# Two-layer decoder trunk on one core: four kinds of small product done another way, four small loads moved, and a new list of issue

## The chip, the core and the metric

The kernel runs on one core of one Trainium2 chip. The metric is the device time of one execution in microseconds (us). The core's engines work side by side, each through its own queue in strict order: TensorE (PE in the profile; PEld is its weight load), VectorE (DVE), ScalarE (ACT), GpSimd (POOL) and SyncE (SP, which here only issues loads and stores). DMA engines move the data between device memory and the core.

## What is computed

256 tokens of width 1024 go through two layers in f32. Cut to what matters:

```python
c_act = silu(c)
for layer in range(2):
    ada = c_act @ w_ada[layer] + b_ada[layer]              # 1024 -> 3 * 1024
    shift, scale, gate = split(ada, 3)
    h = rms_norm(x, norm_g[layer]) * (1 + scale) + shift
    if layer == 0:   # "even": two groups of eight heads
        proj = h @ w_in_even                               # 1024 -> 2840
        oa = sliding_window_attention_with_sinks(...) * silu(za)
        k_cmp, v_cmp = compress_mlp(kc), compress_mlp(vc)  # blocks of 32 tokens, stride 16: 15 blocks
        p_cmp = masked_softmax(q @ k_cmp.T * 64 ** -0.5)   # the compressed scores
        ob = (g0 * (p_cmp @ v_cmp) + g1 * selected_blocks(...) + g2 * window(...)) * silu(zb)
        y = concat(oa, ob) @ w_out_even
    else:            # "odd": sixteen heads; with 256 tokens one block, plain causal attention
        q, k, v, z = split(h @ w_in_odd, 4)                # 1024 -> 4096
        y = (causal_attention(q, k, v) * silu(z)) @ w_out_odd
    x = x + gate * y
return rms_norm(x, final_g)
```

## The kernel before

Tokens are two tiles of 128, the width eight tiles of 128. A projection is done in f32 accuracy with the faster f32r products: ACT casts a weight or an activation to f32r (`whi`, `hhi`, `ghi`), DVE subtracts it from the original to get the rest (`wlo`, `hlo`, `glo`), and `mm3` adds three products (hi·hi, hi·lo, lo·hi). So each weight tile of 128x512 costs an ACT cast, a DVE subtraction and PE products. Weights come through a ring of five tiles `raw` of 128x2048, loaded by SP.

Shift, scale and gate of a layer come from `c_act @ w_ada`, in two ways. With n = 2, `ada_sums` lets DVE multiply and add eight k-tiles of 512 columns into `acc` [128x512], whose sum over the 128 partitions is then still to be taken on PE: by `ada_shift_scale` into columns (one value to a partition, `shs`), by `ada_gate` into `gate`, broadcast over all partitions. With n = 1, `ada_rows` takes column-tiled products with `cz` (each column tile of 32 holds one value in its first column) into four partial rows, copied to `asb`, which are then summed over the four on PE. A column-tiled product uses 32 columns of the PE array; four of them run at four places of the array (`tile_position`). There are three n = 2 and two n = 1 jobs of shift and scale for layer 1, three n = 2 gate jobs (one for layer 0, two for layer 1) and two n = 1 gates. Layer 0's shift and scale belong to the start: SP loads pieces of `w_ada` into spare tiles (`qT`, `gate`, `t`), `start_sums` multiplies them on PE by `cz`, ACT copies to `asb`, PE transposes, DVE adds the bias to `shs`, then ACT and DVE scale the normalized, transposed x (`xT` in `bigA`) to `hhi` and `hlo`, and the first projection product can go. `xs` is x, loaded in two halves of 128 tokens; ACT takes each half's mean square, DVE and POOL its root.

`compress()` computes the two small networks of the compressed keys and values: partial sums in four column tiles are copied to `hp`, summed over the four on PE, and copied to `hx`. `cmp_softmax()` takes the scores of all heads against the compressed keys `kcbd`.

The order of all work is written out: `Plan.record` notes every operation with what it depends on, and `issue()` emits them in the order of the list `ORDER`. Each engine does its operations in that order. All operations are issued from one line of `record`, so the profile gives line L257 for all of them, and tiles tell them apart. PSUM has eight banks: three `ps_pj`, two `ps_s`, one each of `ps_pt`, `ps_o` and `ps_m`; the small products of the change all go to the one `ps_m`.

Of the kernel before, what the change touches and what calls it, by code (L numbers as in the profile page):

```python
# [13 lines left out]
P = 128  # L14
D = 1024
S = 256
# [252 lines left out]
def tile_trunk(  # L269
# [192 lines left out]
    def ada_shift_scale(l, g, n, a=None, st=None):  # L462
# [7 lines left out]
        for q in range(2 * n):  # L470
            T.matmul(pc[:, 2 * q : 2 * q + 2], a[:, q * P : (q + 1) * P], st[:, 0:2], start=True, stop=True)
# [902 lines left out]
```

## Time and profile before

| what | value |
|---|---|
| time, median of 3 runs | 305.65 us (305.29 to 306.19) |
| profiled execution | 306.59 us, span 304.8 us |
| PE busy | 292.1 us, 96% of the span |
| DVE busy | 260.4 us, 85% |
| ACT busy | 185.6 us, 61% |
| POOL busy | 10.7 us, 4% |
| DMA | 71.83 MB, mean 236 GB/s |
| granted PE clock | 0.999 |

The span is the profile's; 1.8 us of the profiled execution lie outside it. PE's busy time is modelled from the starts of its pipelined products. The DMA share is the mean busy share of the 16 DMA engines; it can come out a little over 1.

### The profile page before, as it was taken

The numbers are of one execution on the slowest core, as the hardware profiler recorded it, in microseconds if no ns is written. First come the engines' busy times: TensorE is split into PE (matmuls) and PEld (weight loads), VectorE is DVE, ScalarE is ACT, GpSimd is POOL, SyncE is SP. The second block draws the span as 40 slices with busy tenths as digits, with TensorE's granted clock in tenths as the row PEclk, the third lists the DMA queues.
The fourth block names the chain that finished last, engine by engine and source line by source line (L and its number), as shares of the span: only waits on it lengthen the run. The fifth ranks groups of instructions, "written<-read, shape, count | busy, mean of one in ns | idle before, by whom it ended". The sixth has DMA issues, their size and how long they took to land.

```text
span 304.8 us, 6307 instructions
## 1 busy us (share of the span) xinstructions
PE 292.1 (96%) x2303; PEld 250.3 (82%) x2303; DVE 260.4 (85%) x706; ACT 185.6 (61%) x487; POOL 10.7 (4%) x33
## 2 busy tenths in 40 slices
PE   6599999999999999999999999999999999999991
PEld 6478888898788788877877799999789989887891
DVE  0467998999999999999989887778877989999993
ACT  1662464885688978973556844474568258592532
POOL 2400000002000000000020000000000000000010
PEclk9999999999999999999999999999999999999999
DMA  7999999983997775949796958809587565342003
GB/s 253 374 309 366 387 398 378 333 281 98 308 351 236 246 247 165 364 139 301 246 303 214 298 196 268 284 19 326 199 259 236 167 248 153 125 140 69 0 2 139
DMA packets 60926, 71.83 MB, mean 236 GB/s; under 512 B 2840, under 2 KB 52448, under 8 KB 60896
## 3 DMA queue, kind: packets, MB, share of 16 engines
q1 hardware_dynamic: 60320, 70.91, 70.5%
q10 hardware_dynamic: 448, 0.48, 0.5%
q8 instruction: 18, 0.29, 0.4%
q14 instruction: 12, 0.10, 0.1%
q0 software_dynamic: 128, 0.05, 0.1%
HBM read 70.38 MB, written 1.05 MB: 234 GB/s over the span
## 4 chain that ended last, share of the span: by engine, by line
PE 87%; DVE 6%; ACT 3%; DMA 2%; issue 1%; SPq 0%; POOL 0%; ACTq 0%; DVEq 0%
PE ps_pj L257 52%; PE ps_s L257 12%; PE ps_pt L257 8%; PE ps_m L257 8%; PE ps_o L257 7%; DVE t L257 2%; DMA xs<-in_x_dram 2%; DVE wlo L257 2%; ACT t L257 1%; DVE xs L257 1%; ACT whi L257 1%; ACT L257 0%; SPq L257 0%; DVE shs L257 0%; ACT hhi L257 0%
## 5 line engine op out<-in xcount | busy, mean ns | idle before, releaser
L257 ACT CAST whi<-raw 128x512 fp32r<-128x512 f32 (+1 forms) x132 | 74.1, 600 | 19.9 <-PE ps_pj L257 11.9
L257 DVE TENSOR_TENSOR wlo<-raw,whi 128x512 fp32r<-128x512 f32 (+1 forms) x116 | 72.6, 659 | 4.6 <-ACT whi L257 4.6
L257 PE MATMUL ps_pj<-hhi,whi 128*128 128x256 f32 x256 | 68.8, 290 | 0.0
L257 PE MATMUL ps_pj<-hhi,wlo 128*128 128x256 f32 x256 | 67.7, 286 | 0.0
L257 PE MATMUL ps_pj<-hlo,whi 128*128 128x256 f32 x256 | 67.0, 284 | 0.0
L257 PEld LDWEIGHTS ps_pj<-hhi,whi 128*128 128x128 f32 x256 | 46.3, 188 | 1.5 <-issue 0.6
L257 PEld LDWEIGHTS ps_pj<-hhi,wlo 128*128 128x128 f32 x256 | 46.4, 189 | 0.5 <-issue 0.2
L257 PEld LDWEIGHTS ps_pj<-hlo,whi 128*128 128x128 f32 x256 | 46.0, 188 | 1.0 <-issue 0.7
L257 DVE SCALAR_TENSOR_TENSOR acc<-raw,cz,acc 128x512 f32<-128x512 f32 x42 | 31.3, 745 | 0.2
L257 ACT ACTIVATE sm<-sm,mn 128x256 f32<-128x256 f32 (+1 forms) x58 | 26.2, 452 | 8.4 <-DVE mn L257 8.2
L257 DVE SCALAR_TENSOR_TENSOR wlo<-raw,whi 128x512 fp32r<-128x512 f32 x32 | 21.3, 688 | 6.1 <-ACT whi L257 6.1
L257 PE MATMUL ps_pj<-whi,hhi 128*128 128x512 f32 (+2 forms) x72 | 25.8, 375 | 0.6 <-ACT hhi L257 0.6
L257 PE MATMUL ps_pj<-wlo,hhi 128*128 128x512 f32 (+2 forms) x72 | 25.9, 372 | 0.0
L257 PE MATMUL ps_pj<-whi,hlo 128*128 128x512 f32 (+2 forms) x72 | 25.7, 367 | 0.0
L257 PE MATMUL ps_pj<-wlo,ghi 128*128 128x512 f32 (+1 forms) x56 | 20.4, 367 | 0.0
L257 PE MATMUL ps_pj<-whi,ghi 128*128 128x512 f32 (+1 forms) x56 | 20.4, 370 | 0.0
L257 PE MATMUL ps_pj<-whi,glo 128*128 128x512 f32 (+1 forms) x56 | 20.2, 367 | 0.0
L257 ACT COPY pT<-ps_pt 128x384 f32<-128x384 f32 x25 | 11.9, 476 | 12.3 <-PE ps_pt L257 12.1
L257 PE MATMUL ps_pt<-ta,sm 128*128 128x128 f32 x87 | 17.4, 282 | 0.0
L257 PEld LDWEIGHTS ps_pj<-whi,hhi 128*128 128x128 f32 x72 | 13.3, 189 | 2.4 <-ACT hhi L257 1.0
L257 PEld LDWEIGHTS ps_pj<-wlo,hhi 128*128 128x128 f32 x72 | 13.4, 189 | 2.2 <-issue 0.2
L257 PEld LDWEIGHTS ps_pj<-whi,hlo 128*128 128x128 f32 x72 | 13.4, 189 | 1.7 <-DVE hlo L257 0.3
(234 smaller groups left out, 610.6 us busy)
## 6 DMA issues: line engine op xcount, KB each, us to landing
raw<-in_w_in_odd_dram SPq DMA_DIRECT2D x16, 1024.0 KB, 6.0
raw<-in_w_ada_dram SPq DMA_DIRECT2D x28, 512.0 KB, 6.7
raw<-in_w_in_even_dram SPq DMA_DIRECT2D x5, 1024.0 KB, 9.8
raw<-in_w_in_even_dram SPq DMA_DIRECT2D x7, 652.0 KB, 6.5
t<-in_w_ada_dram SPq DMA_DIRECT2D x16, 256.0 KB, 6.1
raw<-in_w_out_even_dram SPq DMA_DIRECT2D x4, 1024.0 KB, 6.7
raw<-in_w_out_odd_dram SPq DMA_DIRECT2D x4, 1024.0 KB, 5.6
qT<-in_w_ada_dram SPq DMA_DIRECT2D x12, 256.0 KB, 7.2
```

The source lines that it names most:

```text
L257: self.ops.append(dict(key=eng.key, deps=deps, fn=lambda: getattr(real, name)(*args, **kw)))
```

## The change

It makes six edits in the code and replaces the list:

1. Four small loads (the rows of `b_ada` and `norm_g`, the position rows of the two compress networks; 24, 8, 8 and 8 KB) go out on ACT's queue instead of POOL's.
2. `ada_shift_scale`, n = 2: four f32 products of `acc` tiles with two columns of ones become four column-tiled f32 products with `acc` as the moving side, a copy on ACT to `asb` and one transpose.
3. `ada_shift_scale`, n = 1: two f32 products with `sel` become two transposes and a DVE reduce over the four partial rows.
4. `ada_gate`, n = 2: one f32 product with `ones` becomes a cast on ACT, a subtraction on DVE and two f32r products with `ones_r`. Hi and rest stand in unused parts of `ghi` and `glo`, for one gate of layer 1 in `hhi` and `hlo`. POOL makes `ones_r` once.
5. `compress`: two f32 products with `sel` and a copy become two transposes and a DVE reduce.
6. `cmp_softmax`: eight f32 products of 32 columns become four column-tiled ones of 256 columns, a copy on ACT, and two transposes.
7. `ORDER` is another list throughout: 3,110 operations instead of 3,093.

```diff
@@ ORDER
-73 23 30 27 998 2 1 8 3 4 0 10 43 44 11 12 13 22 14 5 15 45 16 82 17 77 58 7 18 59 76 46 33 19 48 49 60 79 78 47
+74 23 30 27 999 2 0 8 22 10 11 1 12 13 14 3 4 5 6 7 34 15 76 80 59 35 60 75 79 84 77 36 37 16 78 61 17 44 18 38
...
@@ tile_trunk
-    G.dma_start(rows[16:64, :], b_ada.rearrange("l (k p) -> (l k) p", p=P))
+    A.dma_start(rows[16:64, :], b_ada.rearrange("l (k p) -> (l k) p", p=P))
...
@@ ada_shift_scale
-        st = st if st is not None else ones if n == 2 else sel
-        pc = bank("m")
-        for q in range(2 * n):
-            T.matmul(pc[:, 2 * q : 2 * q + 2], a[:, q * P : (q + 1) * P], st[:, 0:2], start=True, stop=True)
-        pv = pc[:, 0 : 4 * n].rearrange("p (s j e) -> p s j e", s=2, e=2)[:, :, :, 0]
+        if n == 2:
+            pa = bank("m")
+            plan.group([
+                T.matmul(
+                    pa[32 * q : 32 * q + 32, :P],
+                    ones[:, 0:32],
+                    a[:, q * P : (q + 1) * P],
+                    start=True,
+                    stop=True,
+                    tile_position=(0, 32 * q),
+                )
+                for q in range(4)
+            ])
+            asb = sb([P, 2 * P], "asb", 2)
+            A.copy(asb[:, :P], pa[:, :P])
+            pc = bank("m")
+            T.transpose(pc[:, :P], asb[:, :P], ident)
+            pv = pc[:, :P].rearrange("p (s j e) -> p s j e", s=2, e=32)[:, :, :, 0]
+        else:
+            pc = bank("m")
+            for q in range(2):
+                T.transpose(pc[:, q * P : (q + 1) * P], a[:, q * P : (q + 1) * P], ident)
+            fs = sb([P, 2], "fs", 2)
+            V.tensor_reduce(fs, pc[:, 0 : 2 * P].rearrange("p (s q e) -> p s q e", s=2, e=32)[:, :, :, 0], axis=mybir.AxisListType.X, op=ALU.add)
+            pv = fs.rearrange("p (s j) -> p s j", j=1)
...
@@ ada_gate
+        if n == 2:
+            ar = [w_[:, 0:2, :] if l and h else w_[:, 6:8, :] for w_ in ((hhi, hlo) if l and h else (ghi, glo))]
+            ar = [w_.rearrange("p a s -> p (a s)") for w_ in ar]
+            A.copy(ar[0], a)
+            V.tensor_tensor(ar[1], a, ar[0].bitcast(F32), ALU.subtract)
         pc = bank("m")
         if n == 2:
-            T.matmul(pc, ones, a, start=True, stop=True)
+            for e in range(2):
+                T.matmul(pc, ones_r, ar[e], start=e == 0, stop=e == 1)
...
@@ compress
-                T.matmul(ph[:, 32 * j : 32 * j + 32], hp[:, j * P : (j + 1) * P], sel, start=True, stop=True)
+                T.transpose(ph[:, j * P : (j + 1) * P], hp[:, j * P : (j + 1) * P], ident)
             hx = sb([P, 64], "hx", 2)
-            V.tensor_copy(hx, ph[:, :64])
+            V.tensor_reduce(hx.rearrange("p (j b) -> p j b", j=2), ph[:, : 2 * P].rearrange("p (j q b) -> p j b q", j=2, q=4), axis=mybir.AxisListType.X, op=ALU.add)
...
@@ cmp_softmax
+        pq = bank("m")
+        plan.group([
+            T.matmul(pq[32 * j : 32 * j + 32, :S], kcbd[:, j // 2, :], qbT[:, j, :], start=True, stop=True, tile_position=(0, 32 * j))
+            for j in range(4)
+        ])
+        sT = sb([P, 2 * P], "asb", 2)
+        A.copy(sT, pq[:, :S])
         pc = bank("m")
         for t in range(2):
-            for hp_ in range(4):
-                T.matmul(
-                    pc[:, t * P + 32 * hp_ : t * P + 32 * hp_ + 32],
-                    qbT[:, hp_, t * P : (t + 1) * P],
-                    kcbd[:, hp_ // 2, :],
-                    start=True,
-                    stop=True,
-                )
+            T.transpose(pc[:, t * P : (t + 1) * P], sT[:, t * P : (t + 1) * P], ident)
```

What the new list does is seen in the engines' queues. A row is an instruction (line, operation, output <- inputs, size); a number behind a tile's name is its buffer, and the buffers have other numbers after.

The first place is the head of ACT's queue, where `crow` is c, `ta` a table with the identity, `tiny` a step of silu(c), and `r` the mean squares of the two halves of x. Before:

```order
L257 DMA ta<-in_tbl_a_dram 128x160
L257 DMA crow<-in_c_dram 8x128
L257 ACT_TABLE_LOAD
L257 ACTIVATE t_86,r_85<-xs 128x1024
L257 ACTIVATE t_88,r_85<-xs 128x1024
L257 ACTIVATE t_87<-xs,r_85 128x512
L257 ACTIVATE tiny_84<-ps_pt_83 128x8
L257 CAST whi_108<-raw_100 128x512
L257 ACTIVATE t_89<-xs,r_85 128x512
L257 COPY bigA<-ps_s_91 128x4x128
```
After:

```order
L258 DMA crow<-in_c_dram 8x128
L258 DMA ta<-in_tbl_a_dram 128x160
L258 DMA rows<-in_b_ada_dram 48x128
L258 DMA rows<-in_norm_g_dram 16x128
L258 DMA rows_pe<-in_cmp_pe_k_dram 16x128
L258 DMA rows_pe<-in_cmp_pe_v_dram 16x128
L258 ACT_TABLE_LOAD
L258 ACTIVATE t_89,r_86<-xs 128x1024
L258 ACTIVATE tiny_85<-ps_pt_84 128x8
L258 ACTIVATE t_87,r_86<-xs 128x1024
L258 ACTIVATE t_90<-xs,r_86 128x512
L258 ACTIVATE t_88<-xs,r_86 128x512
```
Four loads now stand ahead of the first square (the `ACTIVATE` of 128x1024), silu(c) stands between the two squares and not behind both, and a weight cast (`CAST whi`) that stood between the two scalings of x has gone to a later row. The first square in the list after is of the other half of `xs` than before (`t` and `xs` are named alike for both halves).

SP's queue at the same place. Before:

```order
L257 DMA qT_97<-in_w_ada_dram 128x2x256
L257 DMA xs<-in_x_dram 128x1024 x2
L257 DMA raw_100<-in_w_in_even_dram 128x792
L257 DMA qT_99<-in_w_ada_dram 128x2x256
L257 DMA qT_98<-in_w_ada_dram 128x2x256
L257 DMA gate<-in_w_ada_dram 128x2x256
L257 DMA qT_99<-in_w_ada_dram 128x2x256
L257 DMA qT_97<-in_w_ada_dram 128x2x256
L257 DMA qT_98<-in_w_ada_dram 128x2x256
L257 DMA gate<-in_w_ada_dram 128x2x256
L257 DMA raw_100<-in_w_in_even_dram 128x384
L257 DMA raw_100<-in_w_in_even_dram 128x512
```
After:

```order
L258 DMA qT_98<-in_w_ada_dram 128x2x256
L258 DMA xs<-in_x_dram 128x1024 x2
L258 DMA qT_99<-in_w_ada_dram 128x2x256
L258 DMA gate<-in_w_ada_dram 128x2x256
L258 DMA qT_98<-in_w_ada_dram 128x2x256
L258 DMA qT_100<-in_w_ada_dram 128x2x256
L258 DMA raw_101<-in_w_in_even_dram 128x384
L258 DMA qT_99<-in_w_ada_dram 128x2x256
L258 DMA qT_100<-in_w_ada_dram 128x2x256
L258 DMA gate<-in_w_ada_dram 128x2x256
L258 DMA raw_101<-in_w_in_even_dram 128x512
L258 DMA raw_101<-in_w_in_even_dram 128x792
```
The load of 792 columns of `w_in_even`, third kind in the queue before, now stands behind all eight pieces of `w_ada`.

The second place is PE just ahead of the first adaLN products (`ps_m<-qT,cz` and `ps_m<-gate,cz`); `ps_m<-ones` are products of ones with no use but to keep PE at work, and `ta` is the identity of the transposes. Before (the adaLN products are the next row):

```order
L257 MATMUL ps_s_90<-ta,t_87 128x128 x2
L257 MATMUL ps_s_91<-ta,t_87 128x128 x2
L257 MATMUL ps_m_67<-ones 128x128
L257 MATMUL ps_pt_83<-ta,rows 128x64
L257 MATMUL ps_s_91<-ta,t_87 128x128
L257 MATMUL ps_pj_92<-ta,t_89 128x128
L257 MATMUL ps_s_90<-ta,t_87 128x128
L257 MATMUL ps_pj_92<-ta,t_89 128x128 x2
L257 MATMUL ps_s_91<-ta,t_87 128x128
L257 MATMUL ps_pj_92<-ta,t_89 128x128
L257 MATMUL ps_s_90<-ta,t_87 128x128
L257 MATMUL ps_m_67<-ones 128x128
```
After:

```order
L258 MATMUL ps_pt_84<-ta,rows 128x64
L258 MATMUL ps_m_67<-ones 128x128 x2
L258 MATMUL ps_pj_93<-ta,t_90 128x128 x2
L258 MATMUL ps_m_67<-ones 128x128
L258 MATMUL ps_pj_94<-ta,t_90 128x128 x2
L258 MATMUL ps_s_91<-ta,t_88 128x128 x2
L258 MATMUL ps_pj_93<-ta,t_90 128x128
L258 MATMUL ps_s_91<-ta,t_88 128x128 x2
L258 MATMUL ps_m_67<-qT_98,cz 32x128 x8
L258 MATMUL ps_m_67<-qT_99,cz 32x128 x8
L258 MATMUL ps_m_67<-qT_100,cz 32x128 x8
L258 MATMUL ps_m_67<-gate,cz 32x128 x8
```
Before, twelve transposes of the normalized x (`t`) stand ahead of the adaLN products, after nine; the products of ones stand ahead of the transposes now, and `rows` is transposed ahead of them.

The third place is DVE around layer 0's n = 2 gate (`mn` are minima of scores, `rc` and `mc`, `dc` parts of softmax). Before:

```order
L257 ISA bigA,mn_132<-ps_s_90,tb 128x256
L257 ISA mn_132 128x1
L257 ISA bigA,mn_132<-ps_s_90,tb 128x128
L257 ISA mn_132 128x1
L257 TENSOR_TENSOR t_89<-t_89,mc_159 128x256
L257 TENSOR_SCALAR sm_123<-sm_123,rc_139 128x128
L257 TENSOR_TENSOR gate<-ps_m_67,gate 128x512
L257 ISA bigA,mn_132<-ps_s_91,tb 128x256
L257 ISA mn_132 128x1
L257 TENSOR_TENSOR wlo_112<-raw_104,whi_108 128x512
```
After:

```order
L258 TENSOR_TENSOR glo<-acc_106,ghi 128x512
L258 TENSOR_SCALAR mc_160<-mc_160 128x16
L258 ISA bigA,mn_133<-ps_s_92,tb 128x128
L258 ISA mn_133 128x1
L258 TENSOR_TENSOR t_90<-t_90,mc_160 128x256
L258 TENSOR_TENSOR wlo_114<-raw_105,whi_110 128x512
L258 RECIPROCAL rc_141<-den_138 128x4
L258 ISA bigA,mn_133<-ps_s_92,tb 128x256
L258 ISA mn_133 128x1
L258 TENSOR_REDUCE dc_161<-t_90 128x16
L258 TENSOR_TENSOR rc_141<-rc_141,gt 128x4 x2
L258 TENSOR_TENSOR gate<-ps_m_67,gate 128x512
```
The subtraction `glo<-acc` is new, and `gate<-ps_m` follows eleven rows behind it, with other work of the attention and of the weights between.

More of the change, by code (lines that the diff above doesn't have):

```diff
@@ L329, in tile_trunk @@
     A.dma_start(ta, tbl_a)
-    G.dma_start(rows[16:64, :], b_ada.rearrange("l (k p) -> (l k) p", p=P))
-    G.dma_start(rows[0:16, :], norm_g.rearrange("l (k p) -> (l k) p", p=P))
-    G.dma_start(rows_pe[0:16, :], cmp_pe_k.rearrange("o (i t) d -> (o i) (t d)", t=2))
-    G.dma_start(rows_pe[16:32, :], cmp_pe_v.rearrange("o (i t) d -> (o i) (t d)", t=2))
+    A.dma_start(rows[16:64, :], b_ada.rearrange("l (k p) -> (l k) p", p=P))
+    A.dma_start(rows[0:16, :], norm_g.rearrange("l (k p) -> (l k) p", p=P))
+    A.dma_start(rows_pe[0:16, :], cmp_pe_k.rearrange("o (i t) d -> (o i) (t d)", t=2))
+    A.dma_start(rows_pe[16:32, :], cmp_pe_v.rearrange("o (i t) d -> (o i) (t d)", t=2))
     ident = ta[:, 0:128]
@@ L460, in ada_sums, with ada_shift_scale @@
                 V.scalar_tensor_tensor(a, wk, ck, a, op0=ALU.mult, op1=ALU.add)
-    def ada_shift_scale(l, g, n, a=None, st=None):
+    def ada_shift_scale(l, g, n, a=None):
         gs = slice(g, g + n)
@@ L479, in ada_shift_scale @@
             V.tensor_tensor(shs[:, l, 1, gs], shs[:, l, 1, gs], ng, ALU.mult)
+    ones_r = const([P, P], "ones_r", F32R)
+    G.tensor_copy(ones_r, ones)
     selbc = const([P, P], "selbc")
```

259 rows, old and new, of the table ORDER are left out of this document.

## The prediction

> **What bounds the kernel now.** I read the views from the coarse to the fine: first the chain that ended last, then the waits of PE, then the table of stretches, then the timelines of the places that the change touches. The chain's shares by engine:
>
> ```profile
> PE 87%; DVE 6%; ACT 3%; DMA 2%; issue 1%; SPq 0%; POOL 0%; ACTq 0%; DVEq 0%
> ```
>
> PE carries it. All waits of PE in the whole run (engine, tile, releaser, us in total, times, longest):
>
> ```profile
> PE ps_s L257 <- DVE t L257: 4.7, 1, 4.7
> PE ps_m L257 <- DVE ones L257: 1.1, 1, 1.1
> PE ps_pj L257 <- ACT hhi L257: 0.6, 1, 0.6
> ```
>
> The three lie before the first projection product at 19.82 us (rows below). From there on PE is shown to wait for nothing until its last product. The stretches tell how near the next engine stands. Columns: window, length, then busy us and instructions of PE, PEld, DVE, ACT and POOL, granted clock, DMA share, GB/s.
>
> ```profile
> 0.00:20.00 20.00, 13.48 (x109) 11.55 (x110) 5.01 (x17) 8.32 (x16) 5.32 (x23) 1.00 0.93 318
> 20.00:60.00 40.00, 40.00 (x280) 33.89 (x280) 35.78 (x77) 21.46 (x53) 0.00 (x0) 1.00 1.05 368
> 60.00:152.00 92.00, 92.00 (x790) 75.97 (x789) 90.14 (x305) 69.93 (x212) 1.59 (x3) 1.00 0.77 248
> 152.00:165.00 13.00, 12.92 (x87) 9.27 (x85) 11.65 (x29) 6.91 (x16) 1.82 (x3) 1.00 0.84 262
> 165.00:240.00 75.00, 75.00 (x577) 68.41 (x577) 60.05 (x145) 45.06 (x107) 0.67 (x1) 1.00 0.71 227
> ```
>
> So there are three regimes. Up to 19.8 us PE waits for a chain of loads, norm and adaLN sums. From 60 to 152 us PE is full and DVE idles only 92.00 − 90.14 = 1.9 us: whatever shortens PE there must also shorten DVE, or DVE takes over. From 165 to 240 us DVE idles 15 us and PE alone decides. At the border of the layers, the chain runs through DVE:
>
> ```profile
> 160.13 1.20 DVE wlo L257 x2
> 161.33 1.28 DVE t L257 x4
> ```
>
> **The change, part by part. The start.** The chain of the start, in rows of the chain, of ACT, PE and SP (start us, us, what):
>
> ```profile
> 1.74 6.33 DMA xs<-in_x_dram
> 8.09 1.06 ACT L257 ACTIVATE t<-xs 128x1024 f32<-128x1024 f32 x1 [4.93 <-DMA xs<-in_x_dram]
> 8.08 0.37 SPq L257 DMA_DIRECT2D gate<-in_w_ada_dram  x1
> 10.94 1.11 PE L257 MATMUL ps_s<-ta,t 128*128 128x128 f32 x4 [4.74 <-DVE t L257]
> 18.09 0.27 ACT L257 COPY asb<-ps_m 128x128 f32<-128x128 f32 x1 [2.40 <-PE ps_m L257]
> 19.82 0.50 PE L257 MATMUL ps_pj<-whi,hhi 128*128 128x512 f32 x1 [0.58 <-ACT hhi L257]
> ...
> DMA to landing us min/median/max: 4.2/5.3/6.3
> ```
>
> The last line is of the two loads of `xs`: the one issued second lands at 1.74 + 6.33 = 8.07, the other, with the minimum of 4.2 us and its issue half a microsecond sooner, at about 5.4. Before, ACT's first Square is of the half that lands last; the new list puts the other one first. ACT has six DMA issues and a table load ahead of it (0.45 to 0.62 and 1.28 us here), so I take 6.1 us for its start. From the Square to the first transpose it is 10.94 − 8.09 = 2.85 us, so the first transpose is at about 8.9. From there to the first projection it is 19.82 − 10.94 = 8.9 us before; after, three of twelve x transposes come behind the adaLN products, which takes 3 × 0.21 us (at this place two follow each other in 0.21) off it: 8.3. That gives 17.2, a gain of **2.6 us**. The other leg is the last adaLN tile: SP issued it at 8.08, when the late half of `xs` had landed, and from the products' end (the copy at 18.09) to the first projection it is 1.7 us. With SP's 396 KB load of `raw` put behind the adaLN tiles, the last of them should land before 14.3 (it landed at 14.5), products end by 15, and this leg gives 16.7: not the later one. Bounds: 0 if the loads come no sooner, −3.1 if only this leg counts, and below nothing in the rival on load places.
>
> The four small loads on ACT's queue cost four issues of about half a microsecond, ahead of the first Square; the cover is its wait for `xs` until 5.4, which they and the table load overrun by the 0.7 us already in my 6.1. They are needed late (`rows` by `shs` at the chain's end), and taking them off POOL gives nothing, since POOL is idle.
>
> The Trainium skill, "DMA: Bandwidth & Descriptors", section "Issuing engines are not separate DMA queues", says that loads issued from several engines run on the same 16 DMA engines, and that this saves only issue time. The trace agrees: the share is 0.93 up to 20 us and 1.05 behind. By that rule the move brings no bandwidth, and it is one reason for the rival in which the start gains nothing.
>
> **The products on PE**, priced from start to start, because the ends overlap:
>
> ```profile
> 100.01 1.02 PE L257 MATMUL ps_m<-acc,ones 128*128 128x512 f32 x2
> 100.47 0.68 PE L257 MATMUL ps_pj<-hhi,whi 128*128 128x256 f32 x1
> 100.99 0.28 PE L257 MATMUL ps_pj<-hlo,whi 128*128 128x256 f32 x1
> ...
> 138.89 0.38 PE L257 MATMUL ps_pt<-ta,bigA 128*128 128x128 f32 x2
> 139.11 0.73 PE L257 MATMUL ps_m<-ones,acc 128*128 128x2 f32 x6
> 139.70 0.48 PE L257 MATMUL ps_pj<-whi,ghi 128*128 128x512 f32 x1
> 140.01 0.27 PE L257 MATMUL ps_pt<-ta,bigA 128*128 128x128 f32 x1
> ...
> 160.68 0.51 PE L257 MATMUL ps_m<-ta,asb 128*128 128x2 f32 x4
> 161.04 0.48 PE L257 MATMUL ps_s<-wlo,ghi 128*128 128x512 f32 x1
> ...
> 93.93 0.31 PE L257 MATMUL ps_m<-kcbd,qT 128*128 128x32 f32 x2
> 94.07 0.31 PE L257 MATMUL ps_pt<-ta,sm 128*128 128x128 f32 x1
> ...
> 156.78 1.07 PE L257 MATMUL ps_m<-raw,cz 128*32 128x256 f32 x16
> 157.78 0.50 PE L257 MATMUL ps_s<-whi,ghi 128*128 128x512 f32 x1
> 158.11 0.39 PE L257 MATMUL ps_s<-wlo,ghi 128*128 128x512 f32 x1
> 158.34 0.40 PE L257 MATMUL ps_s<-whi,glo 128*128 128x512 f32 x1
> ...
> 27.87 0.40 PE L257 MATMUL ps_m<-acc,ones 128*32 128x128 f32 x8
> 28.20 0.50 PE L257 MATMUL ps_pj<-wlo,hhi 128*128 128x512 f32 x1
> ```
>
> An f32 product stands as two instructions, an f32r product as one; an f32r product of 512 columns takes 158.34 − 158.11 = 0.23 us, a transpose (139.11 − 138.89) / 2 = 0.11.
>
> - Gate, n = 2, three times: 100.99 − 100.01 = 0.98 less the 0.12 of the projection between them is 0.86 before, 2 × 0.235 = 0.47 after. Saved 3 × 0.39 = 1.2.
> - Sums, n = 2, three times: six instructions take 0.59, so eight 0.79, and the next product comes some 0.1 late: 0.9. After: eight column-tiled ones take 28.20 − 27.87 = 0.33, the product behind them 0.33 instead of 0.23 (157.78 to 158.11), and a transpose 0.11: with 0.05 for the entry 0.6. Saved 3 × 0.3 = 0.9.
> - Sums, n = 1, twice: 0.36 and 0.08 behind, against two transposes of 0.22: 2 × 0.23 = 0.46.
> - Compressed scores, once: eight of 0.14 in a row, or up to 0.2 where a projection follows; I take 1.55 for all. After: half of the 1.00 of the 16-instruction row, 0.10 behind, two transposes: 0.85. Saved 0.7.
> - Compress, twice: two such products of 0.18 against two transposes: 0.3 together.
>
> Together PE loses **3.6 us**, of it 2.8 before layer 1's first projection at 164 us and 0.8 (two gates) behind it. Bounds: 2.2 and 4.2, by giving each column-tiled group a full latency more or none.
>
> The Trainium skill, "TensorEngine Tiling (Array Packing)", section "Key Properties", says that changing the tiling mode drains TensorE, which speaks against the two grouped replacements. The rows agree that something is paid (0.33 instead of 0.23 behind each group). If a whole latency were paid going in and out of all four groups, the 3.6 would be about 2.2, and the PE-bound rival's time 1.4 us later.
>
> **What is added elsewhere**, from groups (the last two numbers: busy us, mean ns) and one stretch of DVE:
>
> ```profile
> L257 DVE COPY hx<-ps_m 128x64 f32<-128x64 f32 x2 | 0.5, 225 | 0.2 <-PE ps_m L257 0.2
> L257 DVE TENSOR_REDUCE dc<-t 128x16 f32<-128x256 f32 x1 | 0.4, 390 | 0.0
> 136.71 1.29 DVE L257 TENSOR_TENSOR wlo<-raw,whi 128x512 fp32r<-128x512 f32 x2
> 137.92 0.75 DVE L257 SCALAR_TENSOR_TENSOR acc<-raw,cz,acc 128x512 f32<-128x512 f32 x1
> L257 ACT CAST ghi<-oT 128x512 fp32r<-128x512 f32 x8 | 5.0, 619 | 3.8 <-DVE oT L257 3.8
> ```
>
> DVE: a subtraction of 128x512 for each gate, 1.21 / 2 = 0.60; each compress swaps a copy for a reduce of 256 elements, +0.17; each n = 1 job gains a reduce of eight elements, of which no row has the size, between 0.15 (the smallest operations) and 0.39, and I take 0.13 of queue time since it is nearest to the smallest. Up to 164 us this is 0.60 + 0.34 + 0.26 = **1.2 us** (between 1.1 and 1.7); behind it 1.2 for two subtractions, which the 15 us of idle DVE time cover (if not: +1.2). ACT gets three casts of 0.62 and four copies of about 0.3, 3 us in all; the cover is ACT's 92.00 − 69.93 = 22 us of idle time in the tight stretch. Behind an added copy the transposes and then `shs` wait, but the shifts and scales of layer 1 are wanted only at 160 us. POOL's one copy is at the start, where POOL is free.
>
> **The sum.** Start −2.6. Up to 164 us PE could follow with another −2.8, but DVE gets 1.2 us more and has 1.9 to spare in the tight stretch; PE reaches the products that DVE waits for sooner, and I let a third of that idle time go, 0.65. So DVE sets +1.2 − 0.65 = +0.55 there, and layer 1 starts 2.05 us earlier. Behind it PE decides: −0.8. Total **−2.85**. The profiled execution took 306.59 us (span 304.8 and 1.8 around it), which makes 303.7; it lies 0.94 above the median of the runs, 305.65, on whose scale I forecast **302.8 us**. About 0.3% is what a measurement of this kernel can tell from no change: 304.73 to 306.57.
>
> **Rivals.**
> 1. *PE decides all the way.* No row shows PE waiting for DVE, and DVE idles 4.2 us in 20–60 besides, so a new list can pack DVE denser by the 4.0 us that would be needed (2.8 + 1.2). Against it: 98% busy in 60–152, and the chain through DVE at 160 us. Then 305.65 − 2.6 − 3.6 = **299.4**.
> 2. *The start gains nothing.* The DMA share is 1.05 from 20 to 60 us; if the in-projection is fed by loads and not by the start, sooner products wait for weights and the 2.6 us come back as waits. Against it: PE shows no wait for a load there. Then 305.65 + 0.55 − 0.8 = **305.4**, no change.
> 3. *Slower: the small loads hold the places of the big ones.* In the rows a load waits for an older one to land: SP's `gate` tile went out at 8.08, right when `xs` had landed, and by the issue times this is the load eight places ahead, counted over SP and ACT. Four small loads on ACT now take places that the adaLN tiles had. If they land 6.3 us after an issue at about 3 (the slower `xs` half is the nearest row, though they are far smaller), the tiles behind them go out at up to 9.5 instead of 4 to 8, the last lands near 17, and the first projection starts at 22.3: +2.5 instead of −2.6, in all 305.65 + 2.5 + 0.55 − 0.8 = **307.9**. For it: DMA is already full there. Against it: ACT's other small load (`ta`) landed in 3.3 us. It decides from a first projection at about 21.0 on.
>
> **Chances.** My forecast 0.50 (its own range 301.6 to 304.0: the start between −2.0 and −3.1, the reduces, the idle time), rival 1 0.20, rival 2 0.18, rival 3 0.12. Faster by over 0.3%: the first two and a little of the third case, 0.74. Within it: 0.14. Slower: 0.12. The range from 299.2 to 305.5 leaves out rival 3 and the lower half of rival 1's spread, under 2 in 10.
>
> **What would show it.** First projection product near 17.2 us (start right), at 19.8 (rival 2, if late), behind 21 (rival 3); ACT's first Square near 6. The gates as two f32r products of 0.23, the sums as groups of 0.33. In 60–152 DVE still at 98% and PE now with waits for DVE of about 2 us in all would confirm that DVE sets; PE at 100% there and DVE idle under 0.5 us in a shorter stretch would be rival 1. Layer 1's first projection near 162. What would make me wrong most easily: the new list may move other work off DVE's tight stretch, or starve PE at a place I have not costed.

## The result, and the profile after

The changed kernel takes **300.78 us** (median; 300.47 to 301.18) against 305.47 for the kernel before, run beside it (305.18 to 306.19): ratio 0.9844, 95% interval 0.9822 to 0.9865, so 4.7 us faster. The forecast was 302.8. Below, a difference in us is the difference of two ratios times 305.5. The profiled execution took 300.67 us, span 298.9.

The shares of the chain, all waits of PE, and the stretches after (columns as in the prediction):

```profile
PE 87%; DMA 7%; DVE 3%; SPq 1%; ACT 1%; issue 1%; ACTq 0%; DVEq 0%
```
```profile
PE ps_pt L258 <- DMA ta<-in_tbl_a_dram: 2.1, 1, 2.1
PE ps_m L258 <- DVE ones L258: 1.0, 1, 1.0
PE ps_s L258 <- ACT hhi L258: 0.5, 1, 0.5
PE ps_m L258 <- ACT asb L258: 0.2, 1, 0.2
```
```profile
0.00:20.00 20.00, 15.93 (x124) 13.20 (x125) 6.59 (x20) 10.09 (x19) 3.29 (x19) 1.00 0.89 304
20.00:60.00 40.00, 40.00 (x284) 33.68 (x284) 36.66 (x78) 21.47 (x56) 0.00 (x0) 1.00 1.07 379
60.00:152.00 92.00, 91.97 (x784) 73.33 (x784) 91.42 (x307) 69.69 (x212) 1.89 (x4) 1.00 0.80 254
152.00:165.00 13.00, 13.00 (x90) 8.97 (x88) 12.96 (x37) 10.33 (x25) 1.88 (x4) 1.00 1.04 346
165.00:240.00 75.00, 74.94 (x594) 69.91 (x594) 61.42 (x145) 44.51 (x103) 0.00 (x0) 1.00 0.68 217
```

PE waits nowhere in the middle, as before, and from 60 to 152 us DVE is now idle for 92.00 − 91.42 = 0.58 us instead of 1.86, from 152 to 165 for 0.04 instead of 1.35. DVE has become denser, not PE.

The run is best told as the distance between landmarks on PE (starts of products, of the last one its end, us). The first row is the execution that the prediction used, the second another profiled execution of the same kernel:

| | first projection | layer 1's first projection | last product | first to layer 1 | layer 1 to last |
|---|---|---|---|---|---|
| before | 19.82 | 163.94 | 298.66 | 144.13 | 134.72 |
| before, again | 18.26 | 162.49 | 297.13 | 144.22 | 134.64 |
| after | 17.25 | 159.33 | 292.94 | 142.08 | 133.62 |

Behind the start, the two executions of before agree to 0.1 us; all of their difference lies ahead of the first projection. After is 2.1 us shorter to layer 1 and 1.0 to 1.1 shorter behind it. The start (rows of ACT, DVE, PE, the chain and SP):

```profile
5.40 1.06 ACT L258 ACTIVATE t<-xs 128x1024 f32<-128x1024 f32 x1 [0.45 <-DMA xs<-in_x_dram]
7.48 0.49 DVE L258 TENSOR_SCALAR t<-xs,r 128x512 f32<-128x512 f32 x1 [0.38 <-POOL r L258]
5.70 0.24 PE L258 MATMUL ps_pt<-ta,crow 8*128 8x8 f32 x1 [2.15 <-DMA ta<-in_tbl_a_dram]
7.87 0.37 PE L258 MATMUL ps_pt<-ta,rows 64*128 64x64 f32 x1
8.17 1.22 PE L258 MATMUL ps_m<-ones 128*128 128x128 f32 x4
9.18 0.64 PE L258 MATMUL ps_pj<-ta,t 128*128 128x128 f32 x2
15.52 0.26 ACT L258 COPY asb<-ps_m 128x128 f32<-128x128 f32 x1
17.25 0.50 PE L258 MATMUL ps_s<-whi,hhi 128*128 128x512 f32 x1 [0.54 <-ACT hhi L258]
1.78 5.27 DMA rows<-in_b_ada_dram
7.07 0.37 SPq L258 DMA_DIRECT2D qT<-in_w_ada_dram  x1
```

The first Square (the `ACTIVATE` of 128x1024) starts at 5.40 and not at 8.09, and the first projection at 17.25. Before, PE waited 4.7 us for `t` ahead of its first transpose of x. After, `t` is ready at 7.97 and PE comes to it only at 9.18, without a wait: the transpose of `rows` and four products of ones stand ahead in its queue, and its long wait (2.1 us) is for `ta`. The last two rows belong together: `rows`, now on ACT's queue, lands at 7.05 and SP's next load goes out at 7.07.

The replaced products on PE, and what DVE got:

```profile
101.63 0.40 PE L258 MATMUL ps_m<-ghi,ones_r 128*128 128x512 f32 x1
101.87 0.27 PE L258 MATMUL ps_pt<-ta,sm 128*128 128x128 f32 x1
102.45 0.40 PE L258 MATMUL ps_m<-glo,ones_r 128*128 128x512 f32 x1
102.68 0.38 PE L258 MATMUL ps_pt<-ta,sm 128*128 128x128 f32 x2
...
149.31 0.43 PE L258 MATMUL ps_m<-acc,ones 128*32 128x128 f32 x8
149.67 0.50 PE L258 MATMUL ps_s<-whi,glo 128*128 128x512 f32 x1
...
95.41 0.64 PE L258 MATMUL ps_m<-qT,kcbd 128*32 128x256 f32 x8
95.97 0.93 PE L258 MATMUL ps_s<-kTb,qT 64*128 64x128 f32 x8
```
```profile
L258 DVE TENSOR_TENSOR glo<-acc,ghi 128x512 fp32r<-128x512 f32 x2 | 1.3, 672 | 0.0
L258 DVE TENSOR_REDUCE hx<-ps_m 128x64 f32<-128x256 f32 x2 | 0.8, 414 | 0.0
L258 DVE TENSOR_REDUCE fs<-ps_m 128x2 f32<-128x8 f32 x2 | 0.3, 168 | 0.0
```

A gate is 0.24 + 0.23 = 0.47 us from start to start, a group of eight sums 0.36, the compressed scores 0.56 and two transposes.

### The profile page after: what moved, and what is told of

Read it like the earlier page. It is cut to its first block, busy times and chain, and to the rows that moved or that the text cites. A ratio compares the mean times of both kernels' runs of the same rounds, so it can differ in the third digit from the quotient of the medians.

```text
span 298.9 us, 6289 instructions
## 1 busy us (share of the span) xinstructions
PE 288.8 (97%) x2292; PEld 245.2 (82%) x2292; DVE 261.8 (88%) x711; ACT 188.3 (63%) x494; POOL 10.2 (3%) x30
## 3 DMA queue, kind: packets, MB, share of 16 engines
HBM read 70.38 MB, written 1.05 MB: 239 GB/s over the span
## 4 chain that ended last, share of the span: by engine, by line
PE 87%; DMA 7%; DVE 3%; SPq 1%; ACT 1%; issue 1%; ACTq 0%; DVEq 0%
PE ps_pj L258 52%; PE ps_s L258 13%; PE ps_pt L258 8%; PE ps_o L258 8%; PE ps_m L258 6%; DMA raw<-in_w_ada_dram 3%; DMA raw<-in_w_in_even_dram 2%; DMA rows<-in_b_ada_dram 2%; SPq L258 1%; DVE t L258 1%; DVE acc L258 1%; ACT whi L258 0%; DVE wlo L258 0%; DVE xs L258 0%; ACTq L258 0%
## 5 line engine op out<-in xcount | busy, mean ns | idle before, releaser
L258 ACT CAST whi<-raw 128x512 fp32r<-128x512 f32 (+1 forms) x132 | 75.2, 601 | 34.7 <-PE ps_pj L258 13.8
L258 DVE TENSOR_TENSOR wlo<-raw,whi 128x512 fp32r<-128x512 f32 (+1 forms) x116 | 74.1, 660 | 7.1 <-ACT whi L258 7.1
L258 PE MATMUL ps_pj<-hhi,whi 128*128 128x256 f32 x256 | 68.0, 287 | 0.1
L258 PE MATMUL ps_pj<-hlo,whi 128*128 128x256 f32 x256 | 67.8, 287 | 0.0
L258 PE MATMUL ps_pj<-hhi,wlo 128*128 128x256 f32 x256 | 66.4, 285 | 0.0
L258 PE MATMUL ps_pj<-whi,hlo 128*128 128x512 f32 (+2 forms) x72 | 24.8, 368 | 0.0
L258 PE MATMUL ps_pt<-ta,sm 128*128 128x128 f32 x87 | 18.1, 280 | 0.0
L258 PEld LDWEIGHTS ps_pt<-ta,sm 128*128 128x128 f32 x87 | 10.9, 140 | 4.7 <-issue 1.3
```

Source lines behind the costliest of these rows:

```text
L258: self.ops.append(dict(key=eng.key, deps=deps, fn=lambda: getattr(real, name)(*args, **kw)))
```

## Experiments

D is the forecast's theory (DVE sets the pace up to layer 1), P is rival 1 (PE decides all the way). A "lag" is the start of one and the same PE instruction in an experiment's trace minus its start in the trace of the kernel it is made from.

**The list and the products, each alone.** The new list with the old products, which stand where the first PE step of their replacement stood (small loads on ACT):

```diff
 ORDER: after's list, without the added operations
 bodies of ada_shift_scale, ada_gate, compress, cmp_softmax: before's
```

> The changed kernel with the new list and the loads on ACT, but all replaced products as they were (gates, sums, compress, scores in f32, no added casts, copies, subtractions or reduces); each stands where the first PE step of its replacement stood. Theory P (PE decides from the first projection on, so every microsecond of PE counts): the changed kernel's 300.8 plus the 3.2 to 3.6 us that the old products cost more, 304.0 to 304.4; PE without waits, DVE idle in the middle up by 2 us or more. Theory D, my forecast's (DVE decides up to layer 1): DVE has 1.2 us less to do there, so 300.8 + 0.8 - 0.6, about 301.0; PE with no more time in the middle than in the changed kernel. Theory L (the list alone made the gain, the products little): 300.8 to 301.5 with PE busy longer and its end unmoved.

Measured: 306.28 us, ratio 1.0038 (1.0016 to 1.006). That is 5.9 us slower than after, and not even faster than before. Stretch, and the compressed scores:

```profile
60.00:152.00 92.00, 91.83 (x775) 74.73 (x773) 88.36 (x301) 67.32 (x206) 1.89 (x4) 1.00 0.77 245
```
```profile
95.47 1.97 PE L257 MATMUL ps_m<-kcbd,qT 128*128 128x32 f32 x16
97.37 0.93 PE L257 MATMUL ps_s<-kTb,qT 64*128 64x128 f32 x8
```

Here DVE has 3.6 us to spare and the kernel is slower all the same, so in this order it is PE's products that cost: D falls. P has the sign right and the size too small: in one row the eight scores take 1.90 us, where they took 1.42 spread between other products in before. All replaced products, from each start to the next, with what the product right behind runs longer than the median of its kind, take 9.1 us in this order, 8.2 in before and 4.6 in after. So the products account for 4.6 of the 5.6 us by which the stretch from the first projection to the last product is longer here than in after.

The old list with the new products (small loads on POOL), with each new operation put behind what it needs:

> The old list and the loads on POOL, with the new products put in by a rule: a group where the first old product stood, its copy half a microsecond of the old trace later, its transposes 1.3 us later, the casts of a gate when its sums are ready. Theory P: 305.5 - 3.2 to 3.6 = 301.9 to 302.3, with the first projection still at 19.8 us; up to 1 us more if a placement by rule makes PE wait. Theory D: 305.5 + 0.55 - 0.8 = 305.2. Theory L: 305.5.

```profile
PE ps_pt L258 <- ACT bigA L258: 0.9, 1, 0.9
PE ps_pj L258 <- DVE wlo L258: 0.9, 2, 0.5
PE ps_pt L258 <- DVE sm L258: 0.8, 1, 0.8
PE ps_m L258 <- ACT asb L258: 0.7, 1, 0.7
```

Measured: 309.91 us, 1.0149 (1.0121 to 1.0177), slower than both kernels, which no theory had. Such waits of PE behind the start stand in neither kernel: shorter products with a copy or a subtraction between them, put into a list that was not searched for them, turn into waits. Part of it in this trace is the clock: behind the waits of 0.9 us (at 99.77) and 0.5 us (at 101.43) the granted clock is 0.50 from 101.9 to 105.2 us, where products of 256 columns follow each other in 0.21 us instead of 0.12. That is some 1.4 us, an estimate from these numbers; the execution took 310.96 us, 1.05 more than the median. Both runs place by rule what a search would place, so they bound what list and products do alone from above and cannot share out the gain.

**The small loads.** After, with its four loads back on POOL:

```diff
-    A.dma_start(rows[16:64, :], b_ada.rearrange("l (k p) -> (l k) p", p=P))
+    G.dma_start(rows[16:64, :], b_ada.rearrange("l (k p) -> (l k) p", p=P))
...
```

> The changed kernel with only the four small loads back on POOL's queue; the list is the same. If the move of the loads itself brings nothing and the start's gain is the list's: 300.8, within 0.3%. If the small loads hold places that SP's loads then wait for (in the changed kernel's trace SP's loads from the fourth on go out as ACT's loads land), SP's loads go out sooner here, and the first projection comes up to 1 us sooner than 17.25: 299.8 to 300.5. If the move is what makes the start short (POOL issues slowly, its loads land in 5 to 6 us): first projection after 18.5 and 302 or more.

Measured: 300.69 us, 0.9849 (0.9821 to 0.9877): the same time as after. In its profile the first projection starts at 15.72, 1.5 us sooner; PE keeps 1.1 to 1.3 us of that lead to 194 us and loses 1.1 at one place:

```profile
182.23 0.37 SPq L258 DMA_DIRECT2D raw<-in_w_ada_dram  x1
182.65 0.50 SPq L258 DMA_DIRECT2D raw<-in_w_in_odd_dram  x1
183.20 0.50 SPq L258 DMA_DIRECT2D raw<-in_w_ada_dram  x1
```
```profile
192.87 0.75 DVE L258 SCALAR_TENSOR_TENSOR acc<-raw,cz,acc 128x512 f32<-128x512 f32 x1 [1.35 <-DMA raw<-in_w_ada_dram]
195.28 0.38 PE L258 MATMUL ps_pj<-hhi,whi 128*128 128x256 f32 x1 [1.14 <-DVE oT L258]
```

A half tile of `w_ada` goes out behind a 1 MB load of `w_in_odd`, DVE waits for it, and PE 1.1 us for DVE.

**That place mended.** `poolloads_swap` is the run above with the half tile issued ahead of the 1 MB load, `after_swap` is after with the swap alone:

```diff
 ORDER (SP's queue: load of w_in_odd, half tile of w_ada)
-... 2079 2331 2080 ... 1986 2320 2012 ...
+... 2079 2320 2331 2080 ... 1986 2012 ...
```

> The changed kernel with the four loads on POOL, and in SP's queue the second half of a w_ada tile (issued at 184.45 us in the changed kernel's trace, landed at 192.9) goes out ahead of the 1 MB load of w_in_odd that stood before it (183.90). With the loads on POOL the first projection came at 15.7 us, but PE waited 1.14 us at 195.3 for a DVE operation behind the sums that need this tile. If this wait is what gives the earlier start back: no wait there, 299.5 to 299.8. If the start of 15.7 was that execution's alone: 300.7, first projection near 17.

> The changed kernel, loads on ACT as it has them, with only the two issues on SP swapped (the half tile of w_ada ahead of the 1 MB load of w_in_odd). In the changed kernel's profile the wait at 195 us is only 0.2 us long, so 300.5 to 300.8; if it is 0.4 or more longer than the same with the loads on POOL (300.14), the four loads on ACT cost that.

Measured: 300.14 us, 0.9811 (0.9788 to 0.9835), and 301.03 us, 0.9837 (0.9808 to 0.9866). In the first, both half tiles go out together, and DVE's step at 192.5 has no wait:

```profile
183.34 0.92 SPq L258 DMA_DIRECT2D raw<-in_w_ada_dram  x2
```
```profile
192.54 0.75 DVE L258 SCALAR_TENSOR_TENSOR acc<-raw,cz,acc 128x512 f32<-128x512 f32 x1
```

From layer 1 to the last product both take 133.13 us against 133.62 in after and 134.56 with the loads on POOL alone. The wait is gone. The first projection started at 17.31 with the loads on POOL and at 18.46 with them on ACT, so the start at 15.72 was not repeated. 300.14 is the lowest median here, but its interval overlaps that of after, so it is not shown to be faster than after. With the swap in both, the loads on ACT come out 0.8 us longer than on POOL; the expectation took 0.4 or more for a cost of the loads on ACT, but these two intervals overlap too, so that cost is indicated and not shown.

**The start.** A further profile of before, with nothing changed:

> The kernel before, unchanged, for a second profile of it: the first profiled execution lay 0.94 us above the median of its runs. If that lateness is in the start (loads), the first projection comes 1 us sooner here and all later distances are as they were; if it is spread over PE, the distance from the first projection to the last product, 278.8 us, is shorter here.

```profile
6.74 1.06 ACT L257 ACTIVATE t<-xs 128x1024 f32<-128x1024 f32 x1 [3.58 <-DMA xs<-in_x_dram]
18.26 0.50 PE L257 MATMUL ps_pj<-whi,hhi 128*128 128x512 f32 x1 [0.58 <-ACT hhi L257]
```

This time the second half of `xs` landed at 6.72 and not at 8.07, and the first projection came 1.56 us sooner. Then the start of the new list alone: before's products, the loads on ACT, the new list to about 70 us and the old one behind.

```diff
 ORDER: after's list up to PE's 390th shared step, before's list from there
```

> The kernel before with its old products; the loads are on ACT, and the new list's order stands up to PE's 390th step that both lists share (about 60 us, where both have done the same PE work); from there on the old list. Theory S1 (the start's gain stands by itself, and is what the two profiles of before give: first projection at 19.8 and 18.3 there, 17.25 after, so 1.4 us on the scale of the medians): 304.0, first projection near 17.3, distance from it to layer 1's first projection unmoved at 144.2. Theory S2 (2.6 as forecast): 302.8. Theory S3 (saturated DMA swallows it): 305.4, PE with waits for loads or casts between 17 and 60 us.

Measured: 306.14 us, 1.0006 (0.9983 to 1.0028), no gain. The first projection started at 17.43, 0.83 us sooner than in the further profile of before. Against that profile the lag is −0.2 us at 60 us, still ahead of the junction, +0.25 behind it and +1.47 at 194 us. So most of the lead is lost before the lists join, where PE waits 0.3 us for `acc`, and the rest where they join. Behind that, PE waits for ACT:

```profile
PE ps_pj L257 <- ACT bigA L257: 1.2, 1, 1.2
```

ACT stood behind the cast of a `w_in_odd` tile that landed at 172.80, 9.6 us after its issue (6.7 us in before's further profile); the cast starts at 172.89, and the profile puts its wait down to PE's products, which end at 172.85, so which of the two held it is not settled. The run brings nothing for these reasons, and does not price the start.

**More work for DVE.** Five weight subtractions of 128x512 between 62 and 150 us are done twice, 5 × 0.6 = 3.0 us, in after and in before:

```diff
-            V.tensor_tensor(lo[:, o:e], raw[:, o:e], hi[:, o:e].bitcast(F32), ALU.subtract)
+            for _ in range(2 if sub[0] in TWICE else 1):
+                V.tensor_tensor(lo[:, o:e], raw[:, o:e], hi[:, o:e].bitcast(F32), ALU.subtract)
```

> The changed kernel with five of its subtractions of 128x512, spread over 62 to 148 us, made twice in place; the second writes the same again. That is 5 x 0.60 = 3.0 us more in DVE's queue in a stretch where it idles 0.6 us. Theory D (DVE decides there): 2.4 to 3.0 longer, 303.2 to 303.8, with PE waiting for DVE. Theory P (PE decides, and DVE runs ahead of PE by enough): at most 1 us longer, 300.8 to 301.8, PE without waits.

> The same in the kernel before: five subtractions between 62 and 148 us twice, 3.0 us more for DVE, which idles 1.9 us there. Theory D: 1.1 to 3.0 longer, 306.5 to 308.4. Theory P: 305.4 to 306.4. If before takes them and after doesn't, the new list has used up the room that DVE had.

Measured: after 304.44 us, 0.996 (0.9934 to 0.9986), before 309.01 us, 1.0099 (1.0071 to 1.0127). That is 3.5 and 3.0 us more than each without. The lag grows in steps behind each doubled subtraction, from 0.8 (62 us) to 3.7 (158 us) and from −1.6 to 1.1. Either kernel pays more work on DVE in full. The profile shows little of it as waits; of PE in after with it, between 60 and 165 us:

```profile
PE ps_pt L259 <- ACT pT L259: 0.6, 1, 0.6
PE ps_o L259 <- ACT t L259: 0.2, 1, 0.2
PE ps_pt L259 <- ACT whi L259: 0.2, 1, 0.2
```

**Less work for DVE, for PE, for both.** In after, the same five subtractions left out (5 × 0.6 = 3.0 us of DVE); 24 of the third products of 256 columns left out between 62 and 121 us (24 × 0.118 = 2.8 us of PE); both. These kernels leave out part of the computation: the rests of five weight tiles, the lo·hi products of 24 steps.

```diff
+            if sub[0] not in LEFT:
                 V.tensor_tensor(lo[:, o:e], raw[:, o:e], hi[:, o:e].bitcast(F32), ALU.subtract)
...
+        if at in TWO and not last:
+            left[0] += 1
+        else:
             T.matmul(o, slo, mhi, start=False, stop=last)
```

> The changed kernel without the five subtractions of 128x512 that the earlier run did twice (62 to 148 us): the products then use an older rest of a weight. DVE has 3.0 us less in the middle. Theory D (DVE alone decides there): 2.4 to 3.0 shorter, 297.8 to 298.4. Theory P (PE alone): unmoved, 300.8. Theory C (the list has fitted the two to each other, each waits for the other in pieces too short to see): 0.3 to 1.5 shorter, 299.3 to 300.5, with DVE idle in 60 to 152 us up by what the time does not fall.

> The changed kernel without 24 f32r products of 256 columns (the third of a triple, so a small part of a projection is missing), between 62 and 121 us: 24 x 0.118 = 2.8 us less for PE in the middle. Theory D: unmoved, 300.8. Theory P: 298.0. Theory C: 0.3 to 1.5 shorter, and the distance that PE loses shows as PE idle time or as longer steps.

> Both leave-outs together: 3.0 us less for DVE and 2.8 less for PE. Theory D: as without the subtractions alone. Theory P: as without the products alone. Theory C: more than the two alone add up to, 2.2 to 2.8 shorter, 298.0 to 298.6.

Measured: 301.64 us, 0.9851 (0.9824 to 0.9878); 300.38 us, 0.9821 (0.9789 to 0.9853); 300.43 us, 0.982 (0.979 to 0.9851). In medians none is told apart from after. Where the time goes is seen in the lag against after:

| lag, us, at | 22 | 62 | 101 | 114 | 158 | 290 |
|---|---|---|---|---|---|---|
| less DVE | 0.09 | 0.07 | 0.04 | 0.95 | 0.91 | 0.98 |
| less PE | 0.76 | 1.53 | 0.34 | 0.41 | 0.41 | 0.17 |
| less of both | 0.77 | 1.04 | −0.21 | −0.12 | −0.26 | −0.74 |
| swap alone | 1.21 | 1.20 | 1.18 | 0.98 | 0.98 | 0.48 |

Less DVE: no gain at all up to 111 us, with three of the five left out by then (at 68, 86 and 104 us) and DVE idle 1.2 us from 60 to 110; then it loses 0.9 by a tile of `w_out_even`, issued 1.0 us sooner than in after (103.98) and landed 0.96 later (111.93):

```profile
60.00:110.00 50.00, 50.00 (x476) 42.29 (x474) 48.80 (x185) 39.44 (x127) 1.89 (x4) 1.00 0.86 268
```
```profile
112.00 0.62 ACT L259 CAST whi<-raw 128x512 fp32r<-128x512 f32 x1 [1.79 <-DMA raw<-in_w_out_even_dram]
113.06 0.55 PE L259 MATMUL ps_pt<-ta,sm 128*128 128x128 f32 x3 [0.94 <-ACT pT L259]
```

Less PE: from 62 to 101 us it gains 1.2 of the 2.0 us that the 17 products left out there are worth, while the swap alone, as late at the start, makes up nothing; then PE meets DVE, and gains little more:

```profile
103.79 0.39 PE L258 MATMUL ps_pj<-hhi,wlo 128*128 128x256 f32 x1 [0.27 <-DVE wlo L258]
```

Both: 1.3 us gained between 62 and 158 of the 2.8. The step at 103 us stays, with the same wait of 0.27 us for `wlo` (at 103.24), though two of the subtractions left out lie ahead of it.

By the last product the run with less PE has gained no more than the swap alone (0.76 to 0.17, and 1.21 to 0.48), so what PE gains in the middle is shown in one profile and not in the time.

## Why the prediction was right and wrong

Faster, and inside the range; outside the forecast's own range of 301.6 to 304.0. The forecast of −2.85 stands against −4.7 measured. In the sum's three terms, against the execution that the prediction used: start −2.6 forecast, −2.57 measured; up to layer 1 +0.55 forecast, −2.05 measured; behind it −0.8 forecast, −1.10 measured, and 0.2 less behind the last product. That is −5.9, in the spans 304.8 − 298.9; the medians differ by 4.7. So on the scale of the medians two terms were wrong, with opposite signs: the start brought less than forecast, the stretch up to layer 1 more. The errors cancel in part: 1.4 us too much for the start, 2.6 too little up to layer 1, 0.5 too little behind it.

**The failed step: "DVE sets +1.2 − 0.65 = +0.55 there".** PE took 2.05 us less there, where the forecast had 0.55 more. From its first to its last product PE took 3.15 us less (275.69 against 278.84 us). The products saved 3.6, as forecast: the replaced ones took 6.44 us from start to start, those in their place 3.86, and the products right behind them ran longer than the median of their kind by 1.76 and 0.70 us in all. Of this, 2.9 fall up to layer 1. So 0.9 us of the saving did not come through there, and that is the most that DVE's added 1.2 us can have cost, if the list brought nothing itself; no run separates the two. The forecast took 98% busy for a limit with a third of 1.9 us to spare; the new list packed DVE by 2.7 us between the first projection and layer 1 (idle 7.37 before, 4.71 after). By the prediction's own test, the waits for DVE of about 2 us that would have confirmed it are absent, and 60–152 us come close to the sign of rival 1 (PE at 100%, DVE idle 0.58 us where it gave under 0.5). Less DVE work brings nothing up to 111 us, and less PE work brings 1.2 us up to 101 us: DVE does not set the time there alone. But the truth in the step is that DVE has no room: 3.0 us more on it costs 3.5 or 3.0, in after and in before, and PE with less to do waits for DVE's `wlo` at 103 us. DVE is fitted just in time for PE; the list can be fitted anew, and was. Rival 1 had this mechanism; its 299.4 carries the start's full 2.6 and the products' full 3.6.

**The start: the number met, by another path than the forecast's.** The first projection came at 17.25 (17.2 forecast), and that agreement is luck. The Square came at 5.40 and not at 6.1: the issues and the table load ahead of it end at 4.95, before its half of `xs` lands at 5.38. The first transpose of x came 3.78 us behind it, not 2.85. In all ten profiles with the new list's start it comes 3.5 us behind PE's product of `crow`, which starts 0.14 us after `ta` has landed, or up to 1.2 us later than that where PE waits for `rows`. So the Square no longer decides, as the forecast had it; it has 1.2 us to spare. From the first transpose to the projection it took 8.07 us (8.3 forecast). And the 2.6 is measured from an execution whose second half of `xs` came late. First projections with before's list: 19.82, 18.26, 18.24, 19.09, mean 18.9; with the new list and the loads on ACT: 17.25, 17.61, 17.33, 18.02, 18.00, 18.46, 17.04, 17.43, mean 17.6; with the loads on POOL 15.72 and 17.31. So the start is worth about 1.2 us on the scale of medians, an estimate from few executions. With −2.05, −1.1 and −0.2 this makes −4.6, against −4.7 measured. The 0.94 us by which the profiled execution lay above the median was all in the term that the change then removed; the prediction subtracted the offset and the term both.

**The late term.** The two subtractions behind layer 1 were covered by DVE's idle time there, as forecast; PE gained 1.1 and not 0.8.

**Prices.** Gate 0.47 (0.47 forecast), group of eight sums 0.36 to the start of the next product (0.33), reduce of eight elements 0.168 busy (0.13 of queue time). For the two grouped replacements, the drain at a change of tiling mode of which the Trainium skill, "TensorEngine Tiling (Array Packing)", "Key Properties", warns is not seen as a full latency in and out: that bound was 2.2, the rows give 3.6.

**Rival 2** (the start gains nothing) is not what happened, but half of its reason is real: a lead from the start is lost later, 1.1 us at a load at 195 us with the loads on POOL, and 0.6 of 0.83 us up to 60 us in the run with the new start only. **Rival 3**'s mechanism is in the trace (SP's load at 7.07 behind `rows` at 7.05). It did not make the kernel slower than before, but it may cost something: from the first transpose to the first projection the two profiles with the loads on POOL take 6.75 and 7.36 us, the eight with them on ACT 7.53 to 8.67. In the time, the loads on POOL or on ACT make 300.69 and 300.78 us, and with the swap 300.14 and 301.03; whether they cost anything there stays open. The Trainium skill, "DMA: Bandwidth & Descriptors", "Issuing engines are not separate DMA queues", has the moved loads change nothing but issue time; the first two times agree with it.

**Open.** How the 3.15 us divide between the products, the list and DVE's added work, since neither list nor products alone were tried in an order searched for it. What stops PE in the run with less of both at 1.3 of 2.8 us. Why a `w_in_odd` load took 9.6 us in the run with the new start only. What the start is worth by itself.

## What to carry to other kernels

A second engine that is 98% busy under a fitted order had no room for more here, and yet did not set the time; a few operations doubled on it and left out on it tell the two apart, and each direction must be asked for itself. A number that comes out as forecast does not show that its path was right: look at which wait ends last. Before an offset between the profiled execution and the median is subtracted, find the term that holds it, with a second profile of the same kernel. Cheaper operations and the order go together: put into an order that was not made for them, they can cost more than they save.

## What was not expected of the hardware

- The start is the varying part: the first projection came between 15.7 and 19.8 us over the profiles here, with the landing of `xs` in the old list and of `ta` and `rows` in the new, while the distances behind it repeat to 0.1 us in two executions of the same kernel.
- Small f32 products cost more in a row than spread: eight scores 1.90 us against 1.42.
- PE can be slowed with little to see: in after with five doubled subtractions the last product lags by 3.3 us, and PE's idle time grows by 1.2 (0.57 to 1.79 up to layer 1). PE's ends are modelled, which may hide the rest; that was not tested.
